# Pooling trunk on one core: fold quarters on interleaved parts, two engines in source order while folding, other load and forming order

## The chip, the cores and the metric

The kernel runs on one core of one Trainium2 chip. Times are microseconds of device time. The core has TensorE (PE; its weight loads are listed apart as PEld), VectorE (DVE), ScalarE (ACT), GpSimd (POOL) and SyncE (SP), whose queue issues most DMAs. Each engine works off its own list of instructions in order; a semaphore holds an instruction until what it needs is done. The time before is the median of 3 runs; the profile is of one further execution.

## The reference

```python
normed = rms_norm(x, norm_w)                       # x: 4096 x 1024
u, gate = split(normed @ in_w, 2)                  # 1024 columns each
pooled = [trailing_mean(u_g, w) - u_g for g, w in enumerate((2, 4, 8, 16))]
mixed = einsum('bsgc,gcd->bsgd', pooled, group_w) + group_b
y = mixed * scale * silu(gate)
h = x + y @ out_w
out = rms_norm(h, final_norm_w)
```

There is one layer, so only the pooling mixer is computed. All is float32.

## The kernel before

*Numbers.* Products of large matrices run on operands split into a high part (ScalarE's copy, L152, with rounding to `fp32r`) and a low part (VectorE's subtraction, L146); `split` makes both. `mm3` (L589) then issues three TensorE passes: high with high, high with low, low with high. A plain float32 matmul is one instruction that the profile lists as two passes.

*Fold.* The means are linear in time, so the group map is first folded into the input weights: v's weights are `in_w[:, :D]` times `group_w` times the norm weight. `fold` (L377) does a quarter of one half `q` of this: two chunks of 128 rows, in one PSUM bank each (`ps2[0]`, `ps2[1]`), 8 matmuls as plain float32, or 24 passes on parts. With parts the columns are interleaved (`woven`), and the eviction puts them back. There are eight quarters: `q` = 0 with k = 0, 4 (plain) and 2, 6 (parts), then `q` = 1 with k = 0, 4, 2, 6 (plain). The quarters alternate between banks 0, 1 and banks 2, 3. Evictions scale by the norm weight (ScalarE L393, L395; VectorE L389).

*Products.* The rows are worked in 4 blocks of 1024, each in two halves of 512. A block's four quarter matrices are multiplied in seven products, P1 to P7, instead of eight (sums S1 to S4 of the rows' quarters, T1 to T4 of the weights' quarters). `steps` lists 4 x 7 products "a" (first half of the channels), 4 x 7 "b", and 8 x 7 "o" (output projection). The sequence is P1, P2, P6, P7, P5, P4, P3 in block 0 and P1, P2, P7, P6, P5, P4, P3 in later "a" blocks. A product is 48 passes of 512 columns into four banks: P1, P2, P7 and P4 go to banks 0 to 3, the others to banks 4 to 7. P1's result is copied to banks 4 to 7 by ScalarE (`copied`), P2 adds onto it in banks 0 to 3 and is evicted with SiLU into two tiles `ev["11"]` (two banks each); P7 starts those banks anew.

*Row factors.* For each half block ScalarE squares and sums four row tiles (L417), takes a root (L193), and a Newton step refines the reciprocal (L197 on). In block 0 VectorE does it, the factors are split (`hl`) and spread over partitions by eight TensorE passes (`spread_rs`, L441) into bank 7, and ScalarE copies that to a tile (`rstd`). In later blocks GpSimd does it, and the factors go through memory (`store_rs` L430, `load_rstd` L461). VectorE multiplies the transposed rows by them (`normalize`, L149).

*Pooling.* When a block's P4 or P3 is done, `pool` computes the windows on VectorE (last step L700) and stores the result to `yd` from SP (L704).

*Tiles.* `take` gives the tile that has been free longest, of two sets (`st`, 11 tiles; `vt`, 8), and `give` returns one, so the sequence of `give` calls in the source decides which tile each later step gets, and so what it waits for. `early` and `early5` are the unused weight buffers of P4, P3 and P5.

*Order.* The tile framework orders instructions on each engine by its own estimate of readiness; `tc.issue_after(x)` holds what follows behind `x` on its engine, `tc.high_priority()` pulls it forward. In the first stage (L1034 to L1156) ten warm-up matmuls run, then the fold, with the spread of block 0's first half in the middle of it, then P1 (`run(0, ...)`), with the spread of the second half among its last passes, then P2. From `n` = 2 a loop loads three steps ahead, forms and splits operands one or two ahead, runs the product and evicts it. ScalarE also issues the saves of block 1's operands (`first_saves`, L485).

Of the kernel before, what the change touches and what calls it, by code (L numbers as in the profile page):

```python
# [15 lines left out]
P = 128  # L16
D = 1024
# [44 lines left out]
def kernel(  # L62
# [78 lines left out]

    def add(dst, a, b):
        nc.vector.tensor_tensor(out=dst, in0=a, in1=b, op=ALU.add)  # L143

    def sub(dst, a, b):
        return nc.vector.tensor_tensor(out=dst, in0=a, in1=b, op=ALU.subtract)  # L146

    def mul(dst, a, b):
        nc.vector.tensor_tensor(out=dst, in0=a, in1=b, op=ALU.mult)  # L149

    def copy(dst, src, func=AF.Copy):
        return nc.scalar.activation(dst, src, func)  # L152
# [38 lines left out]
    def rsqrt(dst, tmp, ms, ss, on_vector=False):  # L191

        root = nc.scalar.activation(tmp, ss, AF.Sqrt, bias=eps, scale=1.0 / D).ins  # L193
# [3 lines left out]
        nc.vector.reciprocal(out=dst, in_=tmp)  # L197
        if on_vector:
            mul(tmp, dst, ms)
            mul(tmp, tmp, dst)  # L200
            nc.vector.tensor_scalar(
                out=tmp, in0=tmp, scalar1=-0.5, scalar2=1.5, op0=ALU.mult, op1=ALU.add
            )
            done = nc.vector.tensor_tensor(out=dst, in0=dst, in1=tmp, op=ALU.mult).ins
            roots.append((root, done))
            return
# [14 lines left out]
    def copy_scaled(dst, u, c):  # L221
        nc.scalar.activation(dst[:, 0], u, AF.Copy, scale=c)
        nc.vector.scalar_tensor_tensor(
            out=dst[:, 1], in0=u, scalar=c, in1=dst[:, 0].bitcast(F32),
            op0=ALU.mult, op1=ALU.subtract,
        )
# [134 lines left out]
    def split_early(place, u, pattern, **sizes):  # L361

        flat = place.rearrange("p s a b -> p s (a b)")
        split(flat, u.rearrange("p a b -> p (a b)" if len(u.shape) == 3 else "p k t c -> p (k t c)"))
        return [flat[:, j].rearrange(pattern, **sizes) for j in range(2)]

    def fold(q, k, g, r, ps2, pool=None, on_vector=False, midway=None):

        pairs = [(r, g)] if not isinstance(r, list) else [(r[0], g[0]), (r[0], g[1]), (r[1], g[0])]
        for kk in range(2):  # L370
            if kk == 1 and midway:
                midway()
# [11 lines left out]
        if len(pairs) == 1:  # L384
            give(r)
        o = take(pool=pool)
        for kk in range(2):
            if on_vector and kk == 0:
                nc.vector.tensor_scalar(  # L389
                    out=o[:, kk], in0=ps2[kk], scalar1=norm_c[k + kk], scalar2=None, op0=ALU.mult  # L390
                )
            elif len(pairs) == 1:
                nc.scalar.activation(o[:, kk], ps2[kk], AF.Copy, scale=norm_c[k + kk])  # L393
            else:
                nc.scalar.activation(  # L395
                    o[:, kk].rearrange("p (j s a) -> p j s a", j=2, s=2),
                    ps2[kk].rearrange("p (j a s) -> p j s a", j=2, s=2),
                    AF.Copy, scale=norm_c[k + kk],
                )
        return o  # L400


# [10 lines left out]
    def square_row(b, half, j):  # L413
        if j == 0:
            sums[b, half] = small.tile([P, 4], F32, tag="ss", name=f"ss{b}_{half}")
        u = held.pop((b, half, j))
        nc.scalar.activation(  # L417
            u[:, 0], u[:, 0], AF.Square, accum_out=sums[b, half][:, j : j + 1]
        )
        give(u)  # L420
# [13 lines left out]
    def spread_rs(half, rs):  # L434

        hl = small.tile([P, 2, 4], F32R, tag="hl", name=f"hl{half}")
        split(hl, rs)
# [84 lines left out]
    def form_in(q, b, i):  # L522
# [72 lines left out]
    def product_in(i, t, sets, by_bank, between=None, behind=None):  # L595
# [4 lines left out]
        for n, (h, ct) in enumerate(halves):  # L600
            if between and n in between:
                between[n]()
            c = slice(ct * P, (ct + 1) * P)
            with tc.issue_after(behind) if behind and n == 0 else nullcontext():
# [397 lines left out]
    def run(n, between=None, behind=None):  # L1002
# [5 lines left out]
        else:  # L1008
            product_in(i, split_up.pop(n), sets, i == P1, between, behind)
# [27 lines left out]
    chunks = [(h, k) for h in range(2) for k in (2 * h, 4 + 2 * h)]  # L1037
# [7 lines left out]
    for j in range(3):  # L1045
        load_row(0, 0, j)
# [3 lines left out]
    v0[0] = fold(0, 0, gw[0], ru[0, 0], pairs_of[0], early)  # L1050
    ru[1, 0] = load_wut(1, 0)
    load_row(0, 0, 3)
# [3 lines left out]
    v1[0] = fold(0, 4, gw[0], ru[0, 4], pairs_of[1])  # L1056
    ru[1, 4] = load_wut(1, 4)

    maps = split_early(w[P6][0], gw[0], "p (t c) -> p t c", t=4)
    give(gw[0])  # L1060
    wut_split = []
    for n, k in enumerate((2, 6)):
        wut_split.append(
            split_early(w[P2][n], ru[0, k], "p (k t c) -> p k t c", k=2, t=4)
        )
        give(ru[0, k])
        if n == 0:
            load(0)
            ru[1, 2] = load_wut(1, 2)
# [3 lines left out]
    for j in range(4):  # L1073
        square_row(0, 0, j)
    with tc.high_priority():
        rs = stats(0, 0)
    copy(ident, raw_ident[:, 0, 0:P])
    give(raw_ident)
    v0[1] = fold(0, 2, maps, wut_split[0], pairs_of[2], early)
    v1[1] = fold(0, 6, maps, wut_split[1], pairs_of[3])  # L1080
# [6 lines left out]
    def spread_first():  # L1087
        with tc.high_priority():
            spread_rs(0, rs)

    def second_side(h):

        sub(v0[h], v1[h], v0[h])
# [7 lines left out]
    for n, (h, k) in enumerate(chunks):  # L1101
        o = fold(
            1, k, gw[1], ru[1, k], pairs_of[n], early5, n < 2, spread_first if n == 1 else None
        )
        stores.append((wvd[k // 2], o))
        if n == 1:
            form(0)
            split_step(0)
            first_split = latest_split[0]
            for hh in range(2):  # L1110
                split_scaled(w[P1][hh], g0[hh], pair(norm_c, hh, 0))
            second_side(0)
# [28 lines left out]
    for h in range(2):  # L1141
        for key in ("21", "22"):
            normalize(0, 1, s[key][h])
        sub(s["21"][h], s["11"][h], s["21"][h])
        sub(s["2"][h], s["22"][h], s["21"][h])
        with tc.issue_after(latest_split[0]), tc.issue_after(latest_split[1]):
# [4 lines left out]
    run(1, behind=spread_done[0])  # L1151
    for h in range(2):
        copy(w[P7][h][:, 0], v0[h])
# [9 lines left out]
    def rest_of_first(n):  # L1163

        i = ORDER_IN[n]
        if i == P6:
            w[P5] = new_w(P5)
            for h in range(2):
# [3 lines left out]
                give(t1)  # L1172
                for j, c in enumerate(pair(norm_c, h, 1)):
# [5 lines left out]
        elif i == P7:  # L1179
            w[P4] = new_w(P4)  # L1180
            for h in range(2):
# [34 lines left out]
    for n in range(2, len(steps)):  # L1216
# [31 lines left out]
        if n == 2:  # L1248
# [6 lines left out]
            form_s4(0)  # L1255
            form(n + 2)
# [86 lines left out]
```

## Time and profile before

| | |
|---|---|
| time, median of 3 runs | 915.0 us (914.0 to 915.37) |
| the profiled execution, device time | 913.19 us |
| its span | 911.4 us |
| granted TensorE clock, mean | 0.999 |
| VectorE busy in the first 100 us (ten stretches of 10 us) | 1.3, 4.6, 8.0, 9.0, 9.1, 10.0, 10.0, 9.4, 8.7, 8.5 us |
| memory read, written | 115.45 MB, 60.83 MB |

A line of the work in order of time is: start, us, engine, source line, operation, out<-in, shape, count, and in brackets how long the engine was idle before it and what ended that. Equal instructions that follow each other are one line. PEq, ACTq and SPq are the engines' sequencers, which issue DMAs. Tile numbers are left out.

### The profile page before, as it was taken

What the parts mean: (1) busy time and instruction counts of PE and PEld (TensorE: products, weight loads), DVE (VectorE), ACT (ScalarE), POOL (GpSimd) and SP (SyncE); (2) the same over time, 40 slices, a digit from 0 to 9 for tenths busy, and PEclk for the clock granted to TensorE, in tenths of its full rate; (3) what the DMA queues carried; (4) which work ended last, traced back from release to release, by engine and by line L of the source; (5) the groups of instructions that cost most, each with busy time, mean ns of one, the idle gap of its engine ahead of it and who ended that gap; (6) DMA issues with size and microseconds to landing.
All of it is one profiled execution on the core that took longest, in us unless ns stands there. A gap on an engine that the chain in (4) does not pass through costs nothing.

```text
span 911.4 us, 11229 instructions
## 1 busy us (share of the span) xinstructions
PE 903.0 (99%) x4214; PEld 789.1 (87%) x4214; DVE 703.7 (77%) x769; ACT 458.4 (50%) x741; POOL 49.0 (5%) x130
## 2 busy tenths in 40 slices
PE   9999999999999999999999999999999999999996
PEld 7888888888888888888888888888888888888886
DVE  3898994894998995586686598589888677676675
ACT  6878447447346564346345446554433424324233
POOL 0023001001100000000000000000101101001010
PEclk9999999999999999999999999999999999999999
DMA  9977775667657536015615715645746536356022
GB/s 352 408 307 233 272 252 185 224 230 255 220 205 280 179 142 195 16 64 216 253 46 182 287 70 177 243 150 185 269 164 221 172 121 241 122 192 222 32 93 93
DMA packets 62550, 177.02 MB, mean 194 GB/s; under 512 B 6048, under 2 KB 22816, under 8 KB 62496
## 3 DMA queue, kind: packets, MB, share of 16 engines
q1 hardware_dynamic: 55920, 154.78, 47.9%
q10 hardware_dynamic: 4176, 13.65, 3.8%
q0 software_dynamic: 2400, 7.88, 2.6%
q8 instruction: 33, 0.54, 0.2%
q14 instruction: 21, 0.17, 0.1%
HBM read 115.45 MB, written 60.83 MB: 193 GB/s over the span
## 4 chain that ended last, share of the span: by engine, by line
PE 89%; DVE 5%; DMA 3%; issue 1%; POOL 1%; ACT 1%; DVEq 0%; ACTq 0%; POOLq 0%
PE bank L589 86%; PE bank L377 3%; DVE st L149 1%; DMA sd<-st 1%; DMA vt<-rd 1%; DVE vt L143 1%; DMA rd<-rs 1%; DVE vt L146 1%; DMA early<-in_wut 0%; DVE st L146 0%; DVE op L146 0%; DMA yd<-st 0%; DVE st L700 0%; DVE vt L692 0%; DVE early L146 0%
## 5 line engine op out<-in xcount | busy, mean ns | idle before, releaser
L589 PE MATMUL bank<-op,w 128*128 128x512 f32 x2688 | 581.4, 379 | 0.5 <-DVE op L146 0.4
L589 PEld LDWEIGHTS bank<-op,w 128*128 128x128 f32 x2688 | 507.7, 189 | 73.3 <-DVE op L146 0.8
L589 PE MATMUL bank<-w,op 128*128 128x512 f32 (+1 forms) x1356 | 290.3, 377 | 0.0
L589 PEld LDWEIGHTS bank<-w,op 128*128 128x128 f32 x1356 | 254.6, 189 | 35.8
L146 DVE TENSOR_TENSOR op<-st,op 128x1024 fp32r<-128x1024 f32 x122 | 148.3, 1219 | 76.3 <-ACT op L152 76.2
L152 ACT ACTIVATE op<-st 128x1024 fp32r<-128x1024 f32 x122 | 128.0, 1052 | 139.5 <-PE bank L589 129.9
L152 ACT ACTIVATE op<-vt 128x1024 fp32r<-128x1024 f32 x44 | 46.0, 1053 | 81.6 <-PE bank L589 67.0
L152 ACT ACTIVATE vt<-bank 128x512 f32<-128x512 f32 x98 | 55.9, 592 | 46.0 <-PE bank L589 39.3
L932 DVE TENSOR_TENSOR st<-bank,st 128x512 f32<-128x512 f32 x60 | 41.1, 687 | 29.9 <-PE bank L589 29.7
L146 DVE TENSOR_TENSOR op<-vt,op 128x1024 fp32r<-128x1024 f32 x44 | 53.4, 1221 | 8.6 <-ACT op L152 8.4
L146 DVE TENSOR_TENSOR st<-st,st 128x1024 f32<-128x1024 f32 x33 | 39.8, 1220 | 6.1 <-DMA st<-sd 2.2
L152 ACT ACTIVATE bank<-bank 128x512 f32<-128x512 f32 x48 | 27.6, 579 | 31.8 <-PE bank L589 28.2
L194 POOL TENSOR_SCALAR oms<-oss 128x2 f32<-128x2 f32 x14 | 9.2, 657 | 602.8 <-ACT st L821 596.6
L146 DVE TENSOR_TENSOR w<-st,w 128x1024 fp32r<-128x1024 f32 x22 | 26.6, 1218 | 13.3 <-ACT w L152 13.3
L670 DVE TENSOR_TENSOR_SCAN vt<-vt,bf 128x512 f32<-128x512 f32 x28 | 34.5, 1268 | 0.2 <-ACT vt L152 0.2
L143 DVE TENSOR_TENSOR vt<-bank,vt 128x512 f32<-128x512 f32 (+1 forms) x51 | 33.1, 677 | 2.0 <-PE bank L589 2.0
L932 DVE TENSOR_TENSOR vt<-bank,vt 128x512 f32<-128x512 f32 (+1 forms) x37 | 24.8, 673 | 12.0 <-PE bank L589 11.7
L152 ACT ACTIVATE w<-st 128x1024 fp32r<-128x1024 f32 x22 | 22.9, 1050 | 18.1 <-PE bank L589 15.0
L152 ACT ACTIVATE st<-bank 128x512 f32<-128x512 f32 x32 | 18.8, 595 | 24.5 <-PE bank L589 17.5
L692 DVE SCALAR_TENSOR_TENSOR vt<-vt,vt 128x1024 f32<-128x1024 f32 x24 | 29.1, 1212 | 0.0
L825 DVE SCALAR_TENSOR_TENSOR st<-st,ors,st 128x1024 f32<-128x1024 f32 x17 | 21.4, 1283 | 6.1 <-POOL ors L212 6.1
L149 DVE TENSOR_TENSOR st<-st,vt 128x1024 f32<-128x1024 f32 x21 | 24.7, 1216 | 1.5 <-DMA vt<-rd 1.5
(132 smaller groups left out, 554.6 us busy)
## 6 DMA issues: line engine op xcount, KB each, us to landing
st<-in_x SPq DMA_DIRECT2D x36, 512.0 KB, 5.1
st<-sd SPq DMA_DIRECT2D x28, 512.0 KB, 4.6
st<-in_xt SPq DMA_DIRECT2D x27, 512.0 KB, 6.6
vt<-in_x SPq DMA_DIRECT2D x21, 512.0 KB, 4.6
sd<-st ACTq DMA_DIRECT2D x21, 512.0 KB, 5.3
st<-yd SPq DMA_DIRECT2D x19, 512.0 KB, 4.0
yd<-vt SPq DMA_DIRECT2D x17, 512.0 KB, 2.7
out<-st SPq DMA_DIRECT2D x17, 512.0 KB, 3.6
```

Of the source, the lines that this page charges most:

```text
L143: nc.vector.tensor_tensor(out=dst, in0=a, in1=b, op=ALU.add)
L146: return nc.vector.tensor_tensor(out=dst, in0=a, in1=b, op=ALU.subtract)
L149: nc.vector.tensor_tensor(out=dst, in0=a, in1=b, op=ALU.mult)
L152: return nc.scalar.activation(dst, src, func)
L194: nc.gpsimd.tensor_scalar(out=ms, in0=ss, scalar1=1.0 / D, scalar2=EPS, op0=ALU.mult, op1=ALU.add)
L377: latest[0] = nc.tensor.matmul(ps2[kk][:, j * 256 : (j + 1) * 256], a[:, kk, 2 * j + t, :], maps if len(pairs) == 1 else woven(maps), star ...
L589: latest[0] = nc.tensor.matmul(ps, a, b, start=start and n == 0, stop=stop and n == 2, skip_group_check=True).ins
L670: nc.vector.tensor_tensor_scan(s[:, j, at:end], v[:, j, at:end], v[:, j, at - win : end - win], sums_of[j] if sums_of else 0.0, ALU.add, A ...
L692: nc.vector.scalar_tensor_tensor(out=s[:, :, at : at + H], in0=s[:, :, at : at + H], scalar=1.0 / win, in1=v[:, :, HIST:], op0=ALU.mult, o ...
L825: nc.vector.scalar_tensor_tensor(out=us[j], in0=us[j], scalar=rs[:, j : j + 1], in1=fw[0], op0=ALU.mult, op1=ALU.mult,)
L932: partial["added"] = nc.vector.tensor_tensor(out=dst, in0=src, in1=dst, op=ALU.add).ins
```

## The change

1. Quarters k = 0 and k = 2 of `q` = 1 run on interleaved parts. The second group weights `gw[1]` and `ru[1, 0]`, `ru[1, 2]` are split for it (high part on ScalarE, low part on VectorE) into weight buffers not yet used.
2. While folding (`in_line`), every ScalarE and VectorE instruction made through the helpers is issued behind the one before it in the source. The stage is written out in that sequence, and more evictions go to VectorE.
3. Loads: rows 1 to 3 of block 0's first half go behind the second group weights and `ru[1, 0]`; the four row tiles of the second half go ahead of the two loads for P2 (`load(1)`).
4. The first P1 runs half by half (h, then bank) instead of bank by bank. The second spread goes ahead of its last six passes, and the copies of its first banks stand behind the split of P2's operands.
5. In forming P6, P5 and P4 of block 0, S1 (`form(n + 2)`) goes ahead of S4 (`form_s4(0)`) and of the combination for T4, which moves from P6's to P7's step. `xs[0]["2"]` is given back later. Several operands are held behind earlier ones with `issue_after`.

```diff
+    @contextmanager
+    def lined(engine):
+        made = []
+        before = line_end.get(engine) if in_line[0] else None
+        with tc.issue_after(before) if before else nullcontext():
+            yield made
+        if in_line[0]:
+            line_end[engine] = made[-1].ins
...
-    def split_early(place, u, pattern, **sizes):
+    def high_part(place, u, pattern, **sizes):
         flat = place.rearrange("p s a b -> p s (a b)")
-        split(flat, u.rearrange("p a b -> p (a b)" if len(u.shape) == 3 else "p k t c -> p (k t c)"))
-        return [flat[:, j].rearrange(pattern, **sizes) for j in range(2)]
+        u = u.rearrange("p a b -> p (a b)" if len(u.shape) == 3 else "p k t c -> p (k t c)")
+        copy(flat[:, 0], u)
+        def low_part():
+            sub(flat[:, 1], u, flat[:, 0].bitcast(F32))
+        return [flat[:, j].rearrange(pattern, **sizes) for j in range(2)], low_part
-    def fold(q, k, g, r, ps2, pool=None, on_vector=False, midway=None):
+    def fold(g, r, ps2, halves=(0, 1)):
...
+    def evict_fold(o, k, kk, ps2, is_woven, vector=False):
...
         elif i == P5:
             for h in range(2):
                 add(s["11"][h], s["2"][h], s["11"][h])
-            for u in s.pop("2"):
-                give(u)
+            if q or b:
+                for u in s.pop("2"):
+                    give(u)
...
-            with tc.issue_after(behind) if behind and n == 0 else nullcontext():
+            with tc.issue_after(spread_done[0]) if n == behind else nullcontext():
...
-            product_in(i, split_up.pop(n), sets, i == P1, between, behind)
+            product_in(i, split_up.pop(n), sets, i == P1 and n > 0, between, behind)
...
-    for j in range(3):
-        load_row(0, 0, j)
+    load_row(0, 0, 0)
     gw[1] = load_group_w(1)
...
+    gw1, gw1_low = high_part(w[P7][0], gw[1], "p (t c) -> p t c", t=4)
+    sub(v0[0], v1[0], v0[0])
+    gw1_low()
+    wut_high(1, 0, w[P6][1])
+    wut_low(1, 0)
+    fold(gw0, wut_parts[0, 2], pairs_of[2])
...
-    load(1)
     for j in range(4):
         load_row(0, 1, j, early if j < 3 else None)
+    load(1)
     g1 = [load_rows(gate_w, 4 + 2 * h, 0) for h in range(2)]
     load(2)
+    fold(gw1, wut_parts[1, 0], pairs_of[0])
+    o = [take(pool=early5)]
+    evict_fold(o[0], 0, 0, pairs_of[0], True, True)
+    rs = stats(0, 0)
+    split_rs(0, rs)
+    fold(gw[1], ru[1, 4], pairs_of[1], (0,))
+    wut_high(1, 2, w[P2][0])
+    spread_rs(0)
+    fold(gw[1], ru[1, 4], pairs_of[1], (1,))
+    evict_fold(o[0], 0, 1, pairs_of[0], True, True)
+    wut_low(1, 2)
+    o.append(take(pool=early5))
+    for kk in range(2):
+        evict_fold(o[1], 4, kk, pairs_of[1], False)
+    form(0)
+    split_step(0)
+    first_split = latest_split[0]
+    split_scaled(w[P1][0], g0[0], pair(norm_c, 0, 0))
+    fold(gw1, wut_parts[1, 2], pairs_of[2])
+    o.append(take(pool=early5))
+    evict_fold(o[2], 2, 0, pairs_of[2], True)
+    split_scaled(w[P1][1], g0[1], pair(norm_c, 1, 0))
+    evict_fold(o[2], 2, 1, pairs_of[2], True)
+    fold(gw[1], ru[1, 6], pairs_of[3])
...
+    in_line[0] = False
...
+    second_split = latest_split[1]
...
     def copy_first(c):
         def go():
-            with tc.issue_after(roots[1][0]):
+            with tc.issue_after(second_split):
                 copied.append(copy(banks[4 + c], banks[c]))
         return go
-    def spread_second():
+    def copy_and_spread():
+        copy_first(1)()
         with tc.high_priority():
-            spread_rs(1, rs)
+            split_rs(1, rs)
+        with tc.high_priority():
+            spread_rs(1)
-    run(0, {4: copy_first(0), 6: copy_first(1), 7: spread_second})
+    run(0, {6: copy_first(0), 7: copy_and_spread}, 7)
...
-    run(1, behind=spread_done[0])
+    run(1)
...
+        elif i == P7:
+            w[P4] = new_w(P4)
+            for h in range(2):
                 for j, c in enumerate(pair(norm_c, h, 1)):
                     nc.vector.scalar_tensor_tensor(
                         out=g1[h][:, j], in0=g1[h][:, j], scalar=c, in1=g0[h][:, j],
                         op0=ALU.mult, op1=ALU.subtract,
                     )
                 give(g0[h])
-        elif i == P7:
-            w[P4] = new_w(P4)
-            for h in range(2):
                 split(w[P4][h], g1[h])
                 give(g1[h])
...
-            form_s4(0)
-            form(n + 2)
+            with tc.issue_after(latest_split[0]):
+                form(n + 2)
         if kind == "a" and b == 0:
             with tc.issue_after(latest_split[0]):
                 rest_of_first(n)
+        if n == 2:
+            with tc.issue_after(latest_split[0]):
+                form_s4(0)
+            for u in xs[0].pop("2"):
+                give(u)
```

More of the change, by code (lines that the diff above doesn't have):

```diff
@@ L189, with rsqrt @@
     roots = []
-    def rsqrt(dst, tmp, ms, ss, on_vector=False):
-        root = nc.scalar.activation(tmp, ss, AF.Sqrt, bias=eps, scale=1.0 / D).ins
+    def rsqrt(dst, tmp, ms, ss, first=False):
+        root = copy(tmp, ss, AF.Sqrt, bias=eps, scale=1.0 / D).ins
         nc.gpsimd.tensor_scalar(
@@ L1099, in second_side @@
                 )
[L1101 to L1112, printed above, removed]
+    second_side(0)
     give(gw[1])
```

181 lines of the change are left out of this document (107 added, 74 removed).

## The prediction

> **What bounds the kernel now.** I read the page first, then TensorE's busy time by stretches, then the engines' work in order of time over the first 130 us, where all of the change lies.
>
> ```profile
> span 911.4 us, 11229 instructions
> PE 903.0 (99%) x4214; PEld 789.1 (87%) x4214; DVE 703.7 (77%) x769; ACT 458.4 (50%) x741; POOL 49.0 (5%) x130
> ...
> 4.93:31.83 26.90, 26.90 (x153) 24.45 (x153) 15.66 (x21) 21.46 (x37) 0.19 (x1) 1.00 1.03 405
> ...
> 55.09:129.60 74.51, 74.51 (x344) 64.93 (x344) 70.42 (x76) 45.08 (x71) 12.86 (x21) 1.00 0.74 262
> 129.69:904.40 774.71, 774.71 (x3600) 678.62 (x3600) 593.24 (x635) 368.14 (x596) 32.29 (x98) 1.00 0.50 176
> ```
>
> The columns of a stretch are its length, then busy time (and count) of PE, PEld, DVE, ACT, POOL, the granted clock, the DMA share and GB/s. TensorE is never idle for 774.71 us after 129.69, and a matmul takes 74.51 / 344 = 0.217 us. So the kernel gains only by fewer TensorE passes or by closing the few gaps before 129.69, and any new wait adds in full. VectorE is the second bound: 70.42 of 74.51 us between 55.09 and 129.60.
>
> ```profile
> 0.78 4.04 PE L1034 MATMUL bank<-const-bfloat16-1.0 128*128 128x512 bf16 x10 [0.78 <-PEq L1328]
> 4.93 7.17 PE L377 MATMUL bank<-early,early 128*128 128x256 f32 x32
> 11.75 5.71 PE L377 MATMUL bank<-w,w 128*128 128x256 f32 x48
> 17.30 5.36 PE L377 MATMUL bank<-early,early 128*128 128x256 f32 x24
> 22.30 1.19 PE L441 MATMUL bank<-w,hl 128*128 128x128 f32 x8
> ...
> 31.83 9.42 PE L589 MATMUL bank<-op,w 128*128 128x512 f32 x42
> 41.08 0.23 PE L441 MATMUL bank<-w,hl 128*128 128x128 f32 x1
> ...
> 41.84 0.89 PE L441 MATMUL bank<-w,hl 128*128 128x128 f32 x7
> ...
> 55.09 5.23 PE L589 MATMUL bank<-op,w 128*128 128x512 f32 x23 [0.43 <-DVE op L146]
> ```
>
> The gaps: 0.43 us ahead of 55.09, and 129.60 to 129.69, 0.09 us. That is all there is to close.
>
> **The change, part by part.**
>
> *Two quarters on parts.* Two plain quarters run from 4.93 to 11.75, 3.41 us each; two on interleaved parts from 11.75 to 17.30, 2.78 each. Two more of them save 2 x 0.63 = 1.27 us, and the first product P1 would start at 30.56 instead of 31.83. Each takes a high copy on ScalarE and a low subtraction on VectorE, as do the second group weights: 3 x 1.14 us of VectorE, and four more evictions there (0.66 each), 6.1 us in all. The fold's stretch has 26.90 - 15.66 = 11.2 us of VectorE idle to hide them; were that gone, fold quarter and P1 would start later by the excess. The loads move too: 1 MB of rows now goes behind the second group weights, which at 405 GB/s land 2.6 us sooner and are split by about 16.8, before 17.30. Bytes ahead of the plain fourth pair's load are the same. I take the 1.27 whole; the other bound is none of it.
>
> *P1 half by half (not bank by bank), S1 before S4 and T4, stores.* P1 now needs its second half's operands 24 matmuls (5.2 us) later, which covers them; without it P1 would wait about 1 us. S1 early prepares P5's operands sooner, and TensorE has no gap there to lose; it costs nothing while VectorE's total stays. Pool's queue keeps its sequence of stores.
>
> *Second half's rows sooner.* Four 512 KB rows go ahead of two loads for P2, so rows land some 2.6 us sooner and those two 5.2 us later.
>
> ```profile
> 25.89 1.99 ACT L152 ACTIVATE op<-st 128x1024 fp32r<-128x1024 f32 x2
> ...
> 28.36 2.55 ACT L222 ACTIVATE w<-st,colt 128x512 fp32r<-128x512 f32 x4
> 30.81 1.25 ACT L393 ACTIVATE early<-bank,colt 128x512 f32<-128x512 f32 x2
> ...
> 32.80 1.06 ACT L417 ACTIVATE early<-early 128x1024 f32<-128x1024 f32 x1
> ...
> 33.84 1.05 ACT L417 ACTIVATE early<-early 128x1024 f32<-128x1024 f32 x1
> ...
> 37.33 0.30 ACT L193 ACTIVATE tmp<-ss,eps 128x4 f32<-128x4 f32 x1
> ...
> 37.66 0.18 DVE L197 RECIPROCAL rs<-tmp 128x4 f32<-128x4 f32 x1 [0.75 <-ACT tmp L193]
> 37.94 0.16 DVE L149 TENSOR_TENSOR tmp<-rs,ms 128x4 f32<-128x4 f32 x1
> 38.14 0.16 DVE L149 TENSOR_TENSOR tmp<-tmp,rs 128x4 f32<-128x4 f32 x1
> ...
> 39.76 0.15 DVE L146 TENSOR_TENSOR hl<-rs,hl 128x4 fp32r<-128x4 f32 x1
> ```
>
> But the squares are held by ScalarE, not by the rows. In source order it has, from the end of the sixth quarter (17.30 + 2.78 + 3.41 + 1.0 for the first spread + 0.3 to hand over = 24.8), an eviction 0.57, two operand copies 1.9, weights 4 x 0.64, four more evictions 2.3: it is free at 32.1 against 32.80 now. Squares at 1.04 each put the root at 36.4, the reciprocal at 36.8. Behind it VectorE's order in the built program differs: a normalisation (1.14) stands between the reciprocal and the Newton steps, another inside them, and both operand lows of P2 ahead of the low part of the factor (`hl`). From 36.8: 0.18 + 1.14 + 0.6 + 1.14 + 0.16 + 2.28 + 0.16 gives 42.4; now it ends at 39.91. TensorE reaches that spread after 42 matmuls of P1, 41.08 - 31.83 = 9.25 us: at 39.8. *The change adds a wait of 2.6 us here.* Queued behind it are the last six matmuls of P1 and all of P2. Eight spread passes (0.8) and six matmuls (1.3) later P2 starts at 44.5; now 54.65 - 52 x 0.217 = 43.4. That is +1.1, and the 0.43 gap ahead of P6 goes, since the built order puts P6's first operand four large steps sooner: **+0.7 us** up to P6. Bounds: -1.7 if the factor is there in time, +1.7 if it is a microsecond later.
>
> *VectorE's long chain.* What follows is set by VectorE, and at its end by a tile.
>
> ```profile
> 42.77 0.60 ACT L152 ACTIVATE st<-bank 128x512 f32<-128x512 f32 x1 [0.69 <-PE bank L441]
> ...
> 43.40 1.23 DVE L149 TENSOR_TENSOR vt<-vt,st 128x1024 f32<-128x1024 f32 x1 [0.92 <-ACT st L152]
> ...
> 62.97 2.35 DVE L143 TENSOR_TENSOR st<-early,st 128x1024 f32<-128x1024 f32 x2
> 65.25 1.22 DVE L146 TENSOR_TENSOR early<-st,st 128x1024 f32<-128x1024 f32 x1
> ...
> 75.85 0.17 DVE L197 RECIPROCAL rs<-tmp 128x4 f32<-128x4 f32 x1
> ...
> 80.14 0.57 POOL L430 DMA_DIRECT2D rd<-rs  x1 [0.41 <-POOL rs L212]
> 85.31 0.57 POOL L461 DMA_DIRECT2D vt<-rd  x1 [4.61 <-DMA rd<-rs]
> ...
> 92.13 2.36 DVE L149 TENSOR_TENSOR st<-st,vt 128x1024 f32<-128x1024 f32 x2 [1.50 <-DMA vt<-rd]
> ...
> 124.65 1.41 DVE L700 SCALAR_TENSOR_TENSOR st<-vt,colt,st 128x512 f32<-128x512 f32 x2
> 125.98 2.35 DVE L149 TENSOR_TENSOR st<-st,vt 128x1024 f32<-128x1024 f32 x2
> ```
>
> From 43.40 VectorE works back to back (a large instruction every 1.14 us) to the reciprocal of block 1's first half at 75.85: 32.45 us. In the built order three 0.66 scalings and one weight low fall outside, one operand low comes in: 30.95 us. But it starts with the copy of the spread, which ScalarE now makes behind two weights, three bank copies and another weight, at about 44.5 to 45.1. So 45.1 + 30.95 = 76.05, and one operand's high copy comes behind four squares on ScalarE, 0.6 more: reciprocal at 76.7, **0.85 us later than now**. Bounds: 73.3 (the factor in time, copy done at 41.9, the same 0.5 lost) and 77.4 (ScalarE another 0.7 behind). From there to the end of the pool's last product of block 0's second half (L700, 126.06) the instructions are the same, Pool's steps and the factor's trip through memory between them: 126.9.
>
> ```profile
> 126.09 0.33 SPq L704 DMA_DIRECT2D yd<-st  x1
> ...
> 123.16 0.60 ACT L152 ACTIVATE vt<-bank 128x512 f32<-128x512 f32 x1 [3.67 <-PE bank L589]
> 124.46 0.60 ACT L152 ACTIVATE vt<-bank 128x512 f32<-128x512 f32 x1 [0.70 <-PE bank L589]
> 127.23 1.46 ACTq L485 DMA_DIRECT2D sd<-st  x2
> 129.04 1.09 ACT L152 ACTIVATE st<-bank 128x512 f32<-128x512 f32 x2 [3.99 <-DMA yd<-st]
> ```
>
> Here ScalarE evicts block 1's second product. Its first two banks go to a `vt` tile at 123.16 and 124.46; the last two go to the `st` tile that L704 is storing, and wait 3.99 us for that store, from 126.09 to 129.04. The next product, P7, starts at 129.60 - 12 x 0.217 = 127.0, does two banks, and meets the third just as it comes free: the 0.09 us gap. In the changed kernel tiles are given back in another sequence, and the built program shows the *first* two banks going to that `st` tile, with a wait for that store; ahead of them in ScalarE's queue also stand the two saves (L485), which wait for VectorE's next two normalisations. Now P7 cannot start at all before it: 126.9 + 2.95 for the store + 0.65 for eviction and hand-over = 130.5, against 127.0: **+3.5 us**. TensorE would be there at 127.7 and stand for 2.8. The +0.7 is inside this, not beside it. The saves alone, at 126.9 + 2.3 + 0.4, would let the eviction start at 129.6, so a faster store wins 0.3 at most. Later evictions show no such change of tile against its store, and later products keep their order, so nothing is won back behind it.
>
> Sum, against the profiled execution: 913.19 + 3.5 = 916.7 (span 914.9). The median of the runs shown is 915.0, 1.8 above that execution; on it **918.5**. Bounds of the chain give +2.7 (reciprocal not later) to +4.2: 917.7 to 919.2.
>
> **The rivals.**
>
> *The factor is in time* (not slower, 0.14). If ScalarE and VectorE run the fold so that `hl` is ready at 39.8, the reciprocal comes at 73.3, P7's first bank at 127.1: +0.1, 915.1. For it: slack exists in the fold. Against: the squares alone hold ScalarE for 4.2 us behind the fold's last eviction. It decides from a root before 34.
>
> *It does what it says* (0.04): the 1.27 and both gaps are kept, -1.8, 913.2. It needs the eviction not to wait for that store, and VectorE 5 us ahead at 126.
>
> *The clock falls in the new idle time* (slower still, 0.12). The ten opening matmuls (row 0.78, 4.04 us) take 0.40 us each, twice the later 0.217 at the same width. Were TensorE to fall back after the wait at 127.7, and for as long, 4 us at half speed cost 2.0: 920.5. For it: two waits of 2.6 and 2.8 us, each longer than any now. Against: they are short, and the row ahead of 55.09 shows no slowdown after 0.43 us. The Trainium skill, TensorE: Matmul & The Clock Gate (Part 1: The HAM clock gate), gives the rule: about 3.4 us of idleness returns the array to half its clock, and by it both waits stay just under the limit. No trace of this case has an idle time near it.
>
> **How the numbers follow.** The forecast has 0.70, own range 917.4 to 919.6. About 0.2% (1.8 us) is what a measurement here can tell from no change, so faster means under 913.2 and slower over 916.8. Slower: forecast and clock, 0.82. Same: the factor in time and part of the third case, 0.15. Faster: 0.03. The range 915.0 to 920.6 leaves out the full gain and the far side of the clock case.
>
> **What would show it.** Fold quarters: 96 matmuls of form `w,w`, P1 near 30.6. The factor: a TensorE wait near 40, released by VectorE's `hl`, some 2.6 us. The chain: the reciprocal near 76.7. The tile: ScalarE idle until about 129.9 on the store of `st`, then TensorE starting P7 near 130.5 after 2 to 3 us of idleness, released by ScalarE. I am wrong if that idle time is missing, or if the span grows by gaps behind 131.

## The result and the profile after

The changed kernel takes 922.1 us (median of 6 runs, 921.2 to 924.4), the kernel before 914.4 beside it (913.7 to 915.4): a ratio of 1.0084, 95% interval 1.0071 to 1.0097. The prediction said slower, 918.5; the loss is more than twice what it forecast. The profiled execution took 922.1 us, as the median, while that of before took 913.19, which is 1.2 under its median. So 8.9 us of span have to be explained, 5.4 more than the 3.5 of the prediction's sum.

The page's head, and TensorE's work in order of time (the brackets give its waits and what ended them):

```profile
span 920.3 us, 11261 instructions
...
PE 904.3 (98%) x4230; PEld 789.6 (86%) x4230; DVE 710.0 (77%) x776; ACT 458.8 (50%) x740; POOL 51.6 (6%) x130
```

```profile
11.79 8.39 PE L406 MATMUL bank<-w,w 128*128 128x256 f32 x72
20.92 1.97 PE L406 MATMUL bank<-early,early 128*128 128x256 f32 x8 [0.74 <-DVE tmp L224]
...
25.15 3.03 PE L406 MATMUL bank<-w,w 128*128 128x256 f32 x24
...
31.29 9.42 PE L621 MATMUL bank<-op,w 128*128 128x512 f32 x42
41.51 0.33 PE L472 MATMUL bank<-w,hl 128*128 128x128 f32 x1 [0.81 <-ACT hl L171]
42.75 0.99 PE L472 MATMUL bank<-w,hl 128*128 128x128 f32 x7 [0.91 <-DVE hl L157]
43.58 63.88 PE L621 MATMUL bank<-op,w 128*128 128x512 f32 x295
108.01 1.56 PE L621 MATMUL bank<-op,w 128*128 128x512 f32 x6 [0.54 <-DVE op L157]
110.47 19.48 PE L621 MATMUL bank<-op,w 128*128 128x512 f32 x89 [0.90 <-DVE op L157]
134.29 488.87 PE L621 MATMUL bank<-op,w 128*128 128x512 f32 x2256 [4.34 <-ACT st L171]
```

The fold has its 72 + 24 = 96 matmuls on parts, but P1 starts at 31.29, 0.54 us sooner than before and not 1.27: a plain quarter stood 0.74 us for its load (the row names VectorE, whose work that quarter does not read; the load, issued at 12.17, took 8.7 us and so landed at that moment). The factor is late near 40, in two waits that add up to 1.72. The gap ahead of P6 is gone. Block 1's first product waits twice, 1.44 together, which no step had forecast. And P7 stands for 4.34 us, not 2.8.

The next view is the windows view, with a stretch per row: length, busy time and count of PE, PEld, DVE, ACT and POOL, the granted clock, the DMA share and GB/s.

```profile
134.85:138.25 3.40, 3.40 (x10) 2.70 (x9) 1.85 (x2) 3.40 (x7) 0.00 (x0) 0.51 0.79 249
138.25:141.65 3.40, 3.40 (x17) 3.00 (x16) 2.90 (x3) 1.42 (x2) 0.00 (x0) 1.00 0.21 84
```

Shortly after P7 starts, the granted clock is 0.51 for 3.4 us: about 8 matmuls start where 16 do in the next stretch. That costs 1.7 us. Counted by the starts of the matmuls, the 8.9 us are: P1 earlier, -0.54; the wait for the factor, +2.16; the old gap ahead of P6, -0.70; block 1's first product, +1.98; P7, +4.25; the half clock, +1.69. (A wait counts a few tenths more here than its gap, since the matmuls behind it are slower to come.) Behind 139 nothing differs. This is the split of the profiled execution, whose mean granted clock was 0.996; four of the six runs show 0.993 or 0.994, so they had more half clock than this one stretch, and no trace shows where.

The chain behind P7, from the order of time of VectorE, GpSimd (POOL), ScalarE and the DMA issues:

```profile
77.21 0.17 DVE L218 RECIPROCAL rs<-tmp 128x4 f32<-128x4 f32 x1
...
77.53 0.55 POOL L230 TENSOR_TENSOR tmp<-rs,ms 128x4 f32<-128x4 f32 x1 [2.46 <-DVE rs L218]
...
78.82 5.11 POOL L232 TENSOR_SCALAR tmp<-tmp 128x4 f32<-128x4 f32 x1
79.26 1.22 DVE L157 TENSOR_TENSOR op<-st,op 128x1024 fp32r<-128x1024 f32 x1
80.39 2.36 DVE L157 TENSOR_TENSOR w<-vt,w 128x1024 fp32r<-128x1024 f32 x2
82.66 1.22 DVE L157 TENSOR_TENSOR op<-st,op 128x1024 fp32r<-128x1024 f32 x1
83.80 0.69 DVE L157 TENSOR_TENSOR vt<-bank,vt 128x512 f32<-128x512 f32 x1
...
84.62 0.57 POOL L455 DMA_DIRECT2D rd<-rs  x1 [0.41 <-DMA st<-in_xt]
89.62 0.57 POOL L492 DMA_DIRECT2D st<-rd  x1 [4.43 <-DMA rd<-rs]
...
95.89 2.36 DVE L157 TENSOR_TENSOR st<-st,st 128x1024 f32<-128x1024 f32 x2 [3.30 <-DMA st<-rd]
...
128.48 1.41 DVE L732 SCALAR_TENSOR_TENSOR st<-vt,colt,st 128x512 f32<-128x512 f32 x2
...
129.92 0.33 SPq L736 DMA_DIRECT2D yd<-st  x1
...
131.06 0.33 ACTq L516 DMA_DIRECT2D sd<-st  x1
...
132.19 0.33 ACTq L516 DMA_DIRECT2D sd<-vt  x1
...
133.64 2.07 ACT L171 ACTIVATE st<-bank 128x512 f32<-128x512 f32 x4 [10.30 <-DMA yd<-st]
```

From the reciprocal to the normalisation it takes 18.68 us, where it took 16.28. One Newton step of 128x4 elements took 5.11 us on GpSimd; it ends as VectorE, which ran without a pause from 77.2, comes to an eviction from PSUM. Before, the same step took 1.04 us, and VectorE paused for 1.88 us behind it:

```profile
78.41 1.04 POOL L209 TENSOR_SCALAR tmp<-tmp 128x4 f32<-128x4 f32 x1
```

```profile
81.27 2.36 DVE L146 TENSOR_TENSOR op<-st,op 128x1024 fp32r<-128x1024 f32 x2 [1.88 <-ACT op L152]
```

From the normalisation on the two traces run alike: 34.0 us to the pool's last product. The store of that tile goes out at 129.92, and all four evictions of P2 stand behind it until 133.64. The two saves stand ahead of them in ScalarE's queue, the second until 132.52, so of this wait the store alone makes the last 1.1 us.

### The profile page after: what moved, and what is told of

Its sections match the earlier page's. It is cut to its first block, busy times and chain, and to the rows that moved or that the text cites. A ratio compares the mean times of both kernels' runs of the same rounds, so it can differ in the third digit from the quotient of the medians.

```text
span 920.3 us, 11261 instructions
## 1 busy us (share of the span) xinstructions
PE 904.3 (98%) x4230; PEld 789.6 (86%) x4230; DVE 710.0 (77%) x776; ACT 458.8 (50%) x740; POOL 51.6 (6%) x130
## 4 chain that ended last, share of the span: by engine, by line
PE 86%; DVE 6%; ACT 3%; DMA 3%; issue 2%; SPq 0%; ACTq 0%; DVEq 0%; POOLq 0%
PE bank L621 84%; DVE st L157 2%; DVE vt L157 1%; ACT early L171 1%; DVE op L157 1%; DMA st<-in_x 1%; PE bank L406 1%; DMA st<-rd 1%; ACT w L171 1%; DMA rd<-rs 0%; PE bank L1066 0%; ACT op L171 0%; DMA st<-in_xt 0%; DVE st L732 0%; DVE w L157 0%
## 5 line engine op out<-in xcount | busy, mean ns | idle before, releaser
L157 DVE TENSOR_TENSOR op<-st,op 128x1024 fp32r<-128x1024 f32 x117 | 142.5, 1220 | 66.6 <-ACT op L171 66.6
L171 ACT ACTIVATE op<-st 128x1024 fp32r<-128x1024 f32 x117 | 123.1, 1054 | 137.2 <-PE bank L621 124.5
L171 ACT ACTIVATE op<-vt 128x1024 fp32r<-128x1024 f32 x49 | 51.5, 1053 | 86.2 <-PE bank L621 65.0
L157 DVE TENSOR_TENSOR st<-st,st 128x1024 f32<-128x1024 f32 (+1 forms) x62 | 73.5, 1203 | 12.2 <-DMA st<-sd 4.4
L157 DVE TENSOR_TENSOR op<-vt,op 128x1024 fp32r<-128x1024 f32 x49 | 59.5, 1221 | 19.5 <-ACT op L171 19.4
L171 ACT ACTIVATE vt<-bank 128x512 f32<-128x512 f32 x94 | 53.4, 592 | 38.9 <-PE bank L621 37.1
L171 ACT ACTIVATE st<-bank 128x512 f32<-128x512 f32 x36 | 20.7, 597 | 28.7 <-PE bank L621 16.4
L171 ACT ACTIVATE vt<-vt 128x1024 f32<-128x1024 f32 (+1 forms) x18 | 18.1, 1011 | 24.0 <-DVE vt L157 16.8
L157 DVE TENSOR_TENSOR vt<-vt,vt 128x1024 f32<-128x1024 f32 x23 | 27.8, 1216 | 1.5 <-DMA vt<-rd 1.3
```

Of the source, the lines that this page charges most:

```text
L157: made.append(nc.vector.tensor_tensor(out=dst, in0=a, in1=b, op=op))
L171: made.append(nc.scalar.activation(dst, src, func, **how))
```

## The experiments

Each ran beside the kernel before on the same chip. Short diffs stand against the changed kernel, unless said otherwise.

| kernel | median us | ratio to before, 95% | TensorE's waits of note, us |
|---|---|---|---|
| changed kernel | 922.1 | 1.0071 to 1.0097 | factor 1.72, P1 of block 1 1.44, P7 4.34 |
| e1 before, tiles swapped | 916.8 | 1.0012 to 1.0030 | P7 1.94 |
| e2 free tile first | 916.6 | 1.0013 to 1.0031 | factor 1.72, P1 0.95, P7 0.88 |
| e3 Newton on VectorE | 921.3 | 1.0054 to 1.0084 | factor 1.72, P1 0.90, P7 4.23 |
| e4 factor first | 921.8 | 1.0062 to 1.0096 | P2 0.78, P6 0.35, P1 0.97, P7 4.44 |
| e5 e3 + squares behind | 916.5 | 1.0015 to 1.0037 | factor 2.06, P7 0.96 |
| e6 e5 + free tile | 914.8 | 0.9991 to 1.0009 | factor 1.88 |
| e7 e6 + factor first | 913.4 | 0.9977 to 0.9996 | P2 1.15, P6 0.35, P7 0.22 |
| e8 plain fold | 921.6 | 1.0062 to 1.0092 | factor 0.96, P1 1.22, P7 3.87 |
| e9 squares behind alone | 920.5 | 1.0053 to 1.0083 | factor 1.72, P7 2.53 |
| e10 e7 + P2 by halves | 914.5 | 0.9989 to 1.0006 | P2 0.45, P6 1.30 |
| e11 e7 again | 913.1 | 0.9976 to 0.9994 | P2 0.73, P6 0.35 |
| e12 e7 + plain fold | 914.0 | 0.9984 to 1.0002 | P6 0.78 |

**e1: the kernel before with the two tiles swapped.**

```
 elif i == P2:
     ev["11"] = [take() for _ in range(2)]
+    if b == 1 and q == 0:
+        ev["11"].reverse()
```

> The kernel before with nothing changed but the order of the two tiles into which ScalarE evicts block 1's second product: the first two banks now go to the tile that the pool is storing, the last two to the free one. Theory (the tile matters as in the prediction): the store leaves at 126.1 and lands near 129.0, the first eviction ends near 129.7, P7 starts near 129.7 instead of 127.0, TensorE stands for 2.7 us there, no matmul behind it takes twice its time because the wait is shorter than the 4.3 us after which eight of them did, and the time is 914.4 + 2.6 = 917.0 us. Rival (the tile is harmless, the lateness of VectorE alone sets P7's start): 914.4 us. Rival (any wait of over 2 us brings the half clock): 918.7 us, with eight matmuls at 427 ns.

Measured: 916.8 us, +2.3. TensorE's wait at P7, ScalarE's order of time, and the windows of this kernel:

```profile
PE bank L589 <- ACT vt L152: 1.9, 1, 1.9
```

```profile
128.07 0.33 ACTq L485 DMA_DIRECT2D sd<-st  x1
128.50 0.60 ACT L152 ACTIVATE vt<-bank 128x512 f32<-128x512 f32 x1 [8.17 <-DVE st L149]
129.20 0.33 ACTq L485 DMA_DIRECT2D sd<-st  x1
130.01 1.09 ACT L152 ACTIVATE st<-bank 128x512 f32<-128x512 f32 x2 [0.92 <-DMA yd<-st]
```

```profile
130.12:133.52 3.40, 3.40 (x9) 2.70 (x8) 3.40 (x4) 3.40 (x7) 0.00 (x0) 0.50 0.89 301
133.52:136.92 3.40, 3.40 (x17) 2.99 (x16) 2.47 (x4) 2.03 (x4) 0.00 (x0) 1.00 0.82 277
```

The tile makes a wait at P7, of 1.94 us and not 2.7. It isn't the one described, though. The row that releases P7 is an eviction into the `vt` tile, so P7 now begins with a bank that goes to the free tile and doesn't meet the store first; but that eviction comes behind the first of the two saves, and the save waits for VectorE's normalisation. The saves, which the prediction gave 0.3 us of slack, nearly replace the store. Against the theory, this shorter wait also brings a stretch at a granted clock of 0.50. The runs spread from 915.3 to 917.9, more than those of the kernel before, and their mean granted clocks say why: the four of 915.3 to 916.5 us have 0.998, the six of 916.7 to 917.9 have 0.996, as the one with the trace. One such stretch takes 0.002 from the mean (1.7 of 915 us). So the half clock came in about six executions of ten, and the swap without it costs about 1 us.

**e2: a free tile first.**

```
+    if b == 1 and q == 0:
+        keep[0] = 2
     ev["11"] = [take() for _ in range(2)]
+    if b == 1 and q == 0:
+        keep[0] = 3
```

> The changed kernel with block 1's second product evicted into the tiles that the kernel before takes: the first two banks into a free vt tile, the last two into the st tile being stored. Theory (the tile turns VectorE's lateness into TensorE's wait at P7's first bank): TensorE is at P7 at 129.95; the first bank is free at once, P7 does what it can of its first two banks (1.3 us each) and then meets the third, free near 134.2, so the waits at P7 add up to 1 to 2 us instead of 4.3, in pieces, no matmul runs at half clock, and the time is 922.1 - 2.5 - 1.7 = about 917.5 us. Rival (the two saves in ScalarE's queue hold the evictions just as long, so the tile is worth 1.2 us at most): 919 to 921 us.

Measured: 916.6 us, 5.4 less than the changed kernel. The wait of 4.3 at P7 becomes one of 0.84, in the row below, and one of 0.04, and in the trace no half clock follows.

```profile
PE bank L621 <- ACT vt L171: 0.8, 1, 0.8
```

VectorE's chain is as late as before, but P7 now asks first for a tile that nothing holds and reaches the stored one as it comes free. The rival (the saves hold ScalarE just as long) falls: the built order puts the first eviction ahead of both saves. So the edit changes two things, the tile and the place of the first eviction, and its 5.4 us are not the store's alone. The tile with the order that comes of it is the largest single cause.

**e3: Newton steps on VectorE.** 

```
-    rsqrt(rs, tmp, ms, sums[b, half], b == 0)
+    rsqrt(rs, tmp, ms, sums[b, half], b == 0 or (b, half) == (1, 0))
```

> The changed kernel with the four Newton steps of block 1's first factor on VectorE instead of GpSimd. Theory (one GpSimd step took 5.11 us because VectorE ran beside it without a pause, and that is why the stretch from reciprocal to normalisation took 18.7 us and not 16.3): the factor is ready near 80.6 and its store leaves near 80.7 instead of 84.6, normalisation starts near 92.0 instead of 95.9, the waits of 1.4 us in block 1's first product go, the pool's product ends near 126, P7 starts near 130.3 instead of 134.3 after a wait of about 2 us, no matmul runs at half clock, and the time is 922.1 - 4.0 - 1.7 = about 916.4 us. Rival (the step was long by itself or the trip through memory sets the pace): the store leaves at most 1 us sooner and the time stays within 1 us of 922.1.

Measured: 921.3 us; 5 us of the expected gain are missing. In order of time:

```profile
80.81 0.16 DVE L157 TENSOR_TENSOR rs<-rs,tmp 128x4 f32<-128x4 f32 x1
...
81.37 0.57 POOL L455 DMA_DIRECT2D rd<-rs  x1 [6.10 <-DVE rs L157]
86.11 0.57 POOL L492 DMA_DIRECT2D st<-rd  x1 [4.17 <-DMA rd<-rs]
...
90.72 1.06 ACT L171 ACTIVATE vt<-vt 128x1024 f32<-128x1024 f32 x1 [2.81 <-DMA vt<-in_x]
...
92.72 0.28 ACT L171 ACTIVATE tmp<-ss,eps 128x4 f32<-128x4 f32 x1
...
93.04 0.18 DVE L218 RECIPROCAL rs<-tmp 128x4 f32<-128x4 f32 x1 [3.11 <-ACT tmp L171]
93.13 2.33 DVE L157 TENSOR_TENSOR op<-vt,op 128x1024 fp32r<-128x1024 f32 x2
95.38 2.35 DVE L157 TENSOR_TENSOR st<-st,st 128x1024 f32<-128x1024 f32 x2
```

The step is mended: the factor is ready at 80.97 as expected, and its store leaves 3.25 us sooner. Yet the normalisation starts at 95.38, only 0.5 sooner. VectorE now stands for the reciprocal of block 1's *second* half, which comes ahead of the normalisation in its order, as do two operand lows; that reciprocal waits for a root, the root for a square, the square for a row's load. A second bound lay 0.5 us behind the first.

**e4: the factor first.**

```
-    form(1)
     with tc.high_priority():
         rs = stats(0, 1)
+        split_rs(1, rs)
+    factor_split = latest_split[0]
+    with tc.issue_after(roots[1][1]):
+        form(1)
-    with tc.issue_after(roots[1][0]):
+    with tc.issue_after(factor_split):
         split_step(1)
 ...
-        with tc.high_priority():
-            split_rs(1, rs)
```

> The changed kernel with VectorE's order behind the reciprocal mended: the Newton steps and the low part of the second half's factor (hl) ahead of the normalisations and of the low parts of P2's operands. Theory (the wait near 40 us is VectorE's order): hl is ready near 39.6, TensorE does not wait for it, P2 starts 1.7 us sooner; behind it VectorE's chain is 1 to 1.5 us earlier, the wait ahead of P7 and the half clock stay, and the time is 922.1 - 1.5 = 920.6 us. Rival (the root comes too late whatever VectorE's order is): a wait of over 1 us stays near 40 us and the time is 921.5 to 922.5. Rival (P2's own operands are late instead, because their low parts now come behind): the same 1.7 us reappears as a wait ahead of P2.

Measured: 921.8 us, against 920.6 expected. The wait for `hl` goes; of it 0.78 comes back ahead of P2, as the third case had it. P7 starts 1.4 us sooner, at 132.9, but its wait is 4.44 and the half clock lasts longer:

```profile
133.00:139.00 6.00, 6.00 (x14) 4.77 (x15) 4.34 (x5) 5.28 (x9) 0.00 (x0) 0.50 0.71 234
```

14 matmuls at half speed instead of 8 give 1.3 us back. So the wait near 40 is VectorE's order, as the prediction said, and costs nothing by itself while P7 waits for something else.

**e5 and e9: the second bound.** Both issue the last two squares and the factor of block 1's second half behind P3's split and block 1's first normalisation; e5 also has e3's edit, e9 has not.

```
+    def squares_now():
 ...
+    behind_form = b == 0 and i == P4
+    if not behind_form:
+        squares_now()
 ...
     form(n + 2)
+    if ahead and behind_form:
+        with tc.issue_after(latest_split[0]), tc.issue_after(latest_split[1]):
+            squares_now()
```

> The kernel with Newton steps on VectorE, and also with the last squares and the factor of block 1's second half issued behind P3's operand split and block 1's first normalisation. Theory (with GpSimd's long step gone, the normalisation waited for the second half's reciprocal and two operand lows ahead of it in VectorE's order, and these for a row that landed at 90.6): the normalisation starts when the first factor is back, near 93.6 instead of 95.4, the waits in block 1's first product fall from 1.5 us to under 0.5, the pool's product ends near 127.8 instead of 129.8, P7 starts near 131.5; its wait stays above 3 us because TensorE is there sooner too, so the half clock stays, and the time is 921.3 - 1.8 = 919.5 us. Rival (the pool's own work on VectorE between 97 and 130, not the normalisation's start, sets the pool's end): 921.3 us, P7 at 133.6.

> The changed kernel with only the last squares and the factor of block 1's second half issued behind P3's split and block 1's first normalisation; the Newton steps of the first factor are on GpSimd again. Theory (two things each held the normalisation to 95.4 to 95.9 us, the long GpSimd step by way of the factor, the second half's reciprocal by way of VectorE's order, and both have to go): a GpSimd step of 4 to 5 us is still there, the factor is back near 95.5, normalisation starts there, and the time stays within 1 us of 922.1. Rival (the order alone did it and GpSimd's step was harmless): 916.5 us as with both.

Measured: e5 916.5 us, e9 920.5. Alone, Newton on VectorE is worth 0.7 us by the medians and the order 1.6, and the intervals of both overlap that of the changed kernel; together they are worth 5.5. The normalisation's row in e5, then GpSimd's step and the same row in e9:

```profile
92.35 2.36 DVE L157 TENSOR_TENSOR st<-st,st 128x1024 f32<-128x1024 f32 x2 [0.57 <-DMA st<-rd]
```

```profile
78.80 5.11 POOL L232 TENSOR_SCALAR tmp<-tmp 128x4 f32<-128x4 f32 x1
...
94.34 2.36 DVE L157 TENSOR_TENSOR st<-st,st 128x1024 f32<-128x1024 f32 x2 [2.15 <-DMA st<-rd]
```

With both, the normalisation starts at 92.35, 15.3 us behind its reciprocal at 77.01. P7 waits 0.96 for the store instead of 4.34, and no half clock follows; that is why e5 gained more than the 1.8 expected, which had kept a wait of over 3 us there. In e9 the same GpSimd step takes 5.11 us again; its gain of 1.6 is more than the 1 us that the theory allowed; block 1's first product no longer waits, and P7 waits 2.53. Neither rival holds alone: each of the two things was enough to keep the normalisation late.

**e6, e7, e11: all mended.** The edits of e5, e2 and then e4 together.

> The same with the free vt tile for the first two banks of block 1's second product. Theory (the tile turns lateness into a wait, lateness itself costs TensorE only what P7's third bank meets): the waits at P7 add up to under 1 us, no half clock there, block 1's first product without waits of note, and the time is 916.6 - 1.5 = about 915.1 us. Rival (the waits in block 1's first product come from something else than the late normalisation): 916.6 us.

> The same again with the second half's factor ahead of P2's operand lows in VectorE's order. Theory: the wait for hl near 40 us (1.7 us) becomes one of about 0.8 us ahead of P2, as it did when this was done alone, VectorE's chain is 1 us sooner, and the time is 0.4 to 1.2 us under that of the kernel without it: 914.0 to 914.7 us, about the time of the kernel before (914.5). Rival (all that the change saves in the fold comes through once the waits are gone): 913.2 us.

> The kernel with all waits mended, once more beside the next one and in more rounds. Theory: 913.4 us, ratio to the kernel before about 0.9987, as in its first runs; rival (the first runs fell well by chance): 914.5 us, ratio 1.000.

Measured: 914.8, 913.4 and 913.1 us. e6, like e5 and e9, shows that the waits in block 1's first product came from the late normalisation, for they are gone with it. Its runs fall into two groups: five of 913.9 to 914.4 us with a mean granted clock of 0.998 or 0.999, and five of 915.1 to 915.7 with 0.996 or 0.997, among them the one with the trace, which has a stretch at half clock behind the two waits near 40. So part of what e7 gains over e6 is that half clock. e11 is the kernel of e7 once more, and this kernel beats the kernel before: the ratio is 0.9985 (0.9976 to 0.9994), 1.4 us.

**e8 and e12: the fold made plain again**, in the changed kernel and in e7.

```
 ...
-fold(gw1, wut_parts[1, 0], pairs_of[0])
+fold(gw[1], ru[1, 0], pairs_of[0])
 ...
-fold(gw1, wut_parts[1, 2], pairs_of[2])
+fold(gw[1], ru[1, 2], pairs_of[2])
 ...
```

The splits made for these quarters go too, and their evictions become plain ones.

> The changed kernel with its two new quarters on interleaved parts made plain again: no high and low parts of the second group weights and of two weight quarters, 32 plain matmuls in place of 48 faster ones. Theory (up to 130 us VectorE's chain sets the time, not TensorE's work in the fold): P1 starts about 1.2 us later, near 32.5 less what the load waits hide, ScalarE and VectorE have less to do ahead of the chain, P7 starts within 0.5 us of where it did, and the time is within 0.6 us of 922.1. Rival (the saving in the fold reaches the end): 923.3 us.

> The kernel with all waits mended, with the two new quarters of the fold made plain again. Theory (the saving in the fold reaches the end once VectorE's chain no longer holds P7): P1 starts 1.2 us later and the time is 0.6 to 1.2 us longer, 914.0 to 914.6 us. Rival (VectorE's chain still sets P2 and P7): the time is within 0.3 us of the kernel with the quarters on parts, 913.4, with smaller waits ahead of P2 and P7.

Measured: e8 921.6 us, not to be told from the changed kernel; e12 914.0, 0.9 over e11 beside it, with runs of 913.7 to 914.4 against 912.9 to 913.8. In the changed kernel the two faster quarters are worth nothing, because P1's start isn't what P7 waits for. With the waits mended they are worth 0.9 us by the medians. How that reaches the end is not shown: P1 starts at 31.92 in e12's trace, at 31.25 in e11's and at 30.26 in e7's, but the spans of the last two are 911.4 and 911.6, since TensorE waits 0.73 us ahead of P2 in the one and 1.15 in the other.

**e10: P2 by halves.** P2's first operand is normalised and split before the second is normalised (diff against e7).

```
-    with tc.issue_after(roots[1][1]):
-        form(1)
-    with tc.issue_after(factor_split):
-        split_step(1)
 ...
+    for u in xs[0]["12"]:
+        with tc.issue_after(latest_split[0] if split_up[1] else roots[1][1]):
+            normalize(0, 0, u)
+        with tc.issue_after(factor_split):
+            split_up[1] += split_halves([u])
 ...
```

> The kernel with all waits mended, and P2's first operand normalised and split before its second one is normalised. Theory: P2's first half of the weights needs only the first operand, so the wait of 1.15 us ahead of P2 falls to under 0.3, everything to P7 is up to 0.8 us sooner on TensorE, VectorE's chain stays, P7's waits grow by what TensorE gains beyond 0.2 us, and the time is 912.6 to 913.4 us. Rival (P7's third bank meets its store again and takes all of it): 913.4 us, the same as without it.

Measured: 914.5 us, a loss of about 1 us against e7, where a gain was expected. The wait ahead of P2 falls to 0.45, but VectorE pays for the new order ahead of P6, where 1.30 us of waits stand instead of 0.35.

## Why the prediction was wrong

- **The sign and the place were right.** The loss stands where the prediction put it, at P7 of block 1, behind the store of the `st` tile that takes P2's first banks. e2 takes most of the wait out of the changed kernel by another tile, which also puts the first eviction ahead of the saves, for 5.4 us, and e1 makes one at the same place in the kernel before, though by the saves.
- **The fold** was taken whole at 1.27; it gave 0.54 in the changed kernel's trace, the rest lost to one load, and by e8 none of it counted there. "Bytes ahead of the plain fourth pair's load are the same" did not make it land in time: the load took 7.8 us in the trace of before and 8.7 here. In e7's trace it took 7.3, and P1 started at 30.26, 0.3 sooner than forecast.
- **The factor near 40:** `hl` was forecast for 42.4 and ended at 42.69; TensorE came there at 40.70 instead of 39.8, because P1 began later, so the wait was 1.72 and not 2.6. Up to P6 the forecast was +0.7; the rows give -0.54 + 2.16 - 0.70 = +0.9. The later start of P1 only shortened the wait, since `hl` sets where it ends.
- **VectorE's chain, the step that failed:** "From there to the end of the pool's last product of block 0's second half (L700, 126.06) the instructions are the same, Pool's steps and the factor's trip through memory between them: 126.9." The reciprocal came at 77.21 (76.7 forecast, bound 77.4), and the last 34 us were as said, but the stretch between took 18.68 us instead of 16.28: the GpSimd steps and what lies between them up to the store took 7.41 us instead of 4.29, the trip through memory 11.27 instead of 11.99. That VectorE beside it held the long step fits every trace, but no run changed VectorE's work there alone. e3 shows that the factor was 3.3 us late by the GpSimd steps, e5 and e9 that VectorE's order held the normalisation nearly as long by another way. Block 1's first product, which waited on the same chain, was not in the sum at all.
- **The tile's price:** the store took 3.64 us (129.92 to its landing at 133.56) where 2.95 was assumed; two saves went out at 131.06 and 132.19 beside it. By the saves alone the evictions could have started at 132.52, 1.1 us sooner, where the prediction had 0.3. With 0.5, 2.4 and 0.9 us, P7 starts at 134.29 instead of 130.5.
- **The clock:** it was a rival at 0.12, with 2.0 us. It came, with 1.7. The Trainium skill, TensorE: Matmul & The Clock Gate (Part 1: The HAM clock gate), puts the return to half clock at about 3.4 us of idleness, in windows that run free of the kernel. The wait of 4.34 us agrees with that; e1's wait of 1.94 and e9's of 2.53 do not, so reading the page as a limit that the forecast's 2.8 us stays under was wrong.

So of the 8.9 us, 3.5 were forecast; about 3.8 are the chain and the store at P7, and 1.7 the clock. The waits ahead of P7 lie inside these, because the store sets P7's start.

## What to carry to other kernels

Where two engines reach one point within 0.1 us of each other, as TensorE and VectorE did at P7 in the kernel before, a delay of one of them makes a saving on the other worthless there, as e8 shows; mend the later one first, then take the saving. An instruction of a few elements on such a chain need not keep its duration (the GpSimd step took 1.04 to 6.25 us): look for what runs beside it in the new order, not for its old row alone, and look for the second bound close behind the one that the trace names. A tile that goes to the next user while it is still being stored turns a late chain into a wait, and the order in which tiles are given back decides that. A wait of about 2 us can cost 1.7 us more by the clock; here the mean granted clock of each run told when it did.

## What was not expected of the hardware

A GpSimd step on 128x4 elements took 5.11 us in the traces of the changed kernel, e2, e8 and e9, and 6.25 in that of e4, beside VectorE instructions that ran back to back; in the trace of before, where VectorE paused 1.88 us, it took 1.04. The Trainium skill, SBUF — State Buffer (Who interferes with whom), says that a VectorE instruction with two SBUF inputs and a GpSimd instruction that reads SBUF contend for one read interface, and the later one is blocked. The trace agrees that the step ends when VectorE reads PSUM instead (in e9, when VectorE pauses), but it was passed over by four or five VectorE instructions in a row and not by one.

The granted clock fell to half behind waits much shorter than 3.4 us, for about 3.4 us at a time:

```profile
44.60:48.00 3.40, 3.40 (x10) 2.71 (x9) 3.19 (x4) 2.70 (x5) 0.00 (x0) 0.53 1.02 404
133.15:136.55 3.40, 3.40 (x9) 2.70 (x8) 2.03 (x2) 3.40 (x7) 0.00 (x0) 0.50 0.84 231
```

These are two stretches of e9, the first behind the factor's two waits of 0.80 and 0.91 us, the second behind P7's 2.53. The changed kernel had the same two waits near 40, of 0.81 and 0.91, with no such stretch:

```profile
43.60:47.00 3.40, 3.40 (x18) 3.00 (x18) 2.62 (x4) 3.40 (x7) 0.00 (x0) 1.00 1.02 405
```

The traces' record of the clock shows what decides. Between half clocks the full clock lasted whole multiples of 3.413 us in every trace: 129.706 us (38 of them) ahead of the changed kernel's, 37.547 (11) ahead of e5's, 85.333 (25) between the two of e9. So the clock is set anew every 3.413 us, at moments that do not follow the kernel's waits. Counted in these windows from the first rise of the clock, TensorE's idle time in the window just before a half clock was 1.47 (e9, near 40), 1.86 (e6), 1.94 (e1), 2.06 (e5) and 2.50 us (e9, P7), and more in the others. Windows with up to 1.46 us brought none, and two with 1.57 (changed kernel, near 40) and 1.62 us (e3, ahead of P7) brought none either, so the limit lies somewhere between 1.5 and 1.9 us, about half a window, and these traces don't fix it closer. Two short waits near 40 count together when they fall into one window: in e2 and e3, where the end of a window parted them, no half clock came.
